# A decoder layer on one core: turned order of the group stage, one-hots in pairs, heads of a 32-token tile stacked on partitions

## The chip, the core and the metric

The kernel runs on one core of a Trainium2 chip. It is written in a tile framework: the program names operations on tiles, and the framework orders them and sets the semaphores. The metric is the device time of one execution in microseconds (us). Five engines matter. PE (TensorE) multiplies matrices; PEld is its weight load, which lies beside it. DVE (VectorE) does elementwise work and the top-k operations. ACT (ScalarE) does activations and copies with rounding. POOL (GpSimd) does elementwise work too and issues the indirect gathers. SP (SyncE) issues nearly all other transfers, in order. Each engine works through its own queue in order and waits on semaphores of the others.

## The reference, cut to what matters

There are 1056 tokens: 1024 of a prompt and 32 of a sample group (8 sequences of 4). The width is 1024, all in float32, one layer:

```python
z = rmsnorm(x) @ w_in                              # 1024 -> 2304 columns
h = x + concat([rwkv7(z_rwkv), pool_mix(z_pool)]) @ w_out   # 512 + 512 -> 1024
# PEER: product keys, 8 heads, 16 of 16384 single-neuron experts each
q  = (rmsnorm(h) @ wq).reshape(tokens, 8, 2, 128)
s1, s2 = q[:, :, 0] @ sub_keys[0].T, q[:, :, 1] @ sub_keys[1].T   # 128 scores each
v1, i1 = top_k(s1, 16);  v2, i2 = top_k(s2, 16)
sc, ci = top_k((v1[:, None] + v2[None, :]).flatten(), 16)
expert = i1[ci // 16] * 128 + i2[ci % 16];  gate = softmax(sc)
h = h + sum(gelu(u_tab[expert] @ hn) * gate * v_tab[expert])
h = h + (p @ w_ple) * sigmoid(rmsnorm(h) @ w_pg)
y = rmsnorm(h)
```

The RWKV part is a recurrence over the tokens of a sequence, the pooling part is not. Beside y the states are returned.

## The kernel before, in words

Activations lie transposed, width on the 128 partitions and tokens along the free axis. A float32 product of large matrices is done as three products of rounded halves, hi·hi + hi·lo + lo·hi, so each weight and each activation is split once: ACT rounds to hi, DVE or POOL subtracts to lo.

1. `phase_a` (from L189) multiplies the normalised input with the 18 column blocks of w_in. After each of the first products it calls `wsplit` (L176 to L187) twice: this loads four 128x128 blocks of a weight (`sraw`), splits them (`shi` on ACT, `slo` through the helper at L124 on POOL) and stores both to `wc_d` in DRAM. It does so for half of each w_out block (the half of the RWKV columns, 8 pieces) and all of wq (32 pieces), with one buffer for each of the three tiles. The pooling heads end in `yp_d`.
2. `bchunk` (L456 to L639) is the recurrence for 64 tokens; there are 16 such chunks and a sample chunk. Two chunks are in work at a time. A chunk's output goes to `y_d` (L639). `b_stream` runs a range of them.
3. The stage of the sample chunk and chunks 2 and 3. Behind it in program order stand `ple` (L981, the product p @ w_ple into `pl_d`) and `wpool` (L998): the pooled half of the out-projection for all tokens at once, x + w_out's second half times `yp_d`, in 8 blocks of three pieces of 352 columns, stored to `hx_d`.
4. `phase_c` (L682 to L751) for a group of tokens; the groups are 0 to 288, 288 to 544, 544 to 800 and 800 to 1056. It loads y and hx, splits y, adds w_out's RWKV half in 8 blocks (`mm3`, L655 to L664, K of 4 blocks), normalises (L712, L718), multiplies with 16 blocks of wq (K of 8) and with the keys (L747), and stores the scores to `sc_d` (L751). `wblock` (L641) loads the split weights back from `wc_d`, three buffers each of `whi` and `wlo`.
5. `top` and `select` (L753 to L853) for a tile of up to 128 tokens: for each of 8 heads, twice, the 16 best of 128 scores with their indices, then the 16 best of the candidates, codes and gates, with tokens on the partitions. The tokens below 672 are dense tiles: 128, 128 and 32 of group 0, 128 and 128 of group 1, 128 of group 2. For these the gates are spread into a matrix over all 16384 experts. `e12` holds the two halves of the expert's number; they and the gate are transposed (L863); for four tokens at a time a one-hot of each half is made (L875, on DVE, 1024 elements), the second one is multiplied with the gate's upper part (L877, DVE) and its lower part (`GLO`, on POOL for 110 of 168 and else on DVE), and two matmuls a token (L881) make the 128x128 matrix, which goes through `gst` to `g_d` (L884).
6. The remaining 384 tokens are three sparse tiles. Their top-k stands last (L1115). Then 768 gathers of expert rows (L1179) on POOL with a product each on DVE (L1187, L1196) run beside the dense experts: U blocks (`ublock`), gating (`ugate`) and V blocks (`vblock`), all with `esplit` (L1057 to L1064) and `emm` (L1069 to L1075).
7. The per-layer gate, the final norm and the stores.

The order is the program's: the framework plans with priority to what comes first in the program. `merge` interleaves several streams in proportion to given lengths. For the groups a loop (L1089) of four steps merges, in step s, the chunks of BC[s+1:s+3], the top-k and one-hots of group s-2 (`t_stream`), and `phase_c` of group s-1. In the last step `t_stream` of group 2 stands alone, and then `phase_c` of group 3 is merged with seven U blocks done ahead (`upre`).

The lines that the prediction speaks of most:

```python
ab = gp.tile([128, 3, EB, 4], F16, name="ab", bufs=3)               # L874
TT(ab[:, 0:2], iota16[:, None, :, :].to_broadcast([128, 2, EB, 4]), # L875
   e16[:, 0:2, None, t:t + 4].to_broadcast([128, 2, EB, 4]), op=ALU.is_equal)
mm(ps[:, i * 128:(i + 1) * 128], ab[:, k, :, i], ab[:, 0, :, i], start=k == 2, stop=k == 1)  # L881
```

Of the kernel before, what the change touches and what calls it, by code (L numbers as in the profile page):

```python
# [27 lines left out]
PB = 4  # L28
# [23 lines left out]
VG = 8  # L52

# [8 lines left out]
def body(ctx, tc, io):  # L62
# [12 lines left out]
    hx_d = dram.tile([128, KB, T], F32, name="hx_d")  # L75
# [4 lines left out]
    wc_d = dram.tile([KB + 16, 128, 2, KB, 128], F32, name="wc_d")  # L80
    xt_d = dram.tile([GT, D], F32, name="xt_d")
# [559 lines left out]
    def wblock(gi, b):  # L641
# [4 lines left out]
        for i in range(1 if b < KB else 2):  # L646
# [35 lines left out]
    def phase_c(gi):  # L682
# [7 lines left out]
        y = work.tile([128, 4, maxn], F32, name="y", tag="yp")  # L690
        nc.sync.dma_start(y[:, :, :n], y_d[:, :, c0:c1])
# [61 lines left out]
    def top(tk, pos, m):  # L753
        V12 = tk.tile([128, HEADS, 2, TOPK], F32, name="V12", bufs=1)
        I12 = tk.tile([128, HEADS, 2, TOPK], U32, name="I12", bufs=1)
# [13 lines left out]
        yield from select(tk, pos, m, V12, I12)  # L769


    def select(tk, col, m, V12, I12):
        NSL = HEADS * TOPK
        F12 = tk.tile([128, HEADS, 2, TOPK], F32, name="F12")
        for i in range(2):
            ACT(F12[:m, :, i, :], I12[:m, :, i, :], AF.Copy, scale=1.0 if i else 128.0)
        cand = tk.tile([128, HEADS, NCAND], F32, name="cand")
        code = tk.tile([128, HEADS, NCAND], F32, name="code")
        for src, dst, add in ((V12, cand, TT), (F12, code, PTT)):
            off = 0  # L780
            for a, b, w in SEG:
# [3 lines left out]
                if k == 1:  # L785
                    s1 = s1.to_broadcast([m, HEADS, w])
                elif w == 1:
                    s2_ = s2_.to_broadcast([m, HEADS, k])
                else:
                    o = o.rearrange("p h (k w) -> p h k w", w=w)  # L790
                    s1 = s1[:, :, :, None].to_broadcast([m, HEADS, k, w])
                    s2_ = s2_[:, :, None, :].to_broadcast([m, HEADS, k, w])
                add(o, s1, s2_, op=ALU.add)
                off += k * w
        PTT(code[:m], code[:m], iotaC[:m, None, :].to_broadcast([m, HEADS, NCAND]), op=ALU.add)
        SC = tk.tile([128, HEADS, TOPK], F32, name="SC")
        CI = tk.tile([128, HEADS, TOPK], U32, name="CI")
        s3 = cand
        for hh in range(HEADS):
# [153 lines left out]
    with tc.tile_pool(name="smp", bufs=1) as sp_, tc.tile_pool(name="hx", bufs=1) as hx:  # L953
# [73 lines left out]
        for st in (ple(), wpool()):  # L1027
            for _ in st:
                pass
# [349 lines left out]
```

## Time and profile before

| | |
|---|---|
| median of 3 runs | 3516.12 us (3502.51 to 3521.3) |
| the profiled execution's own time | 3494.25 us |
| its span (first to last instruction) | 3492.4 us |
| PE busy | 3262.7 us, 93% |
| DVE busy | 2675.0 us, 77% |
| POOL busy | 1769.3 us, 51% |
| ACT busy | 1179.8 us, 34% |
| HBM read, written | 759.22 MB, 120.60 MB |

How to read the profile. The page gives totals for each engine, and then the span in 40 slices of 87 us, each digit the busy share in tenths. A row of a group reads: line of the kernel, engine, operation, the tile written, the tiles read, the number of instructions, and then durations (minimum, median and maximum in nanoseconds, or busy microseconds and the mean), first and last start in microseconds, and the forms as partitions x elements. In the page's own group rows the last column is the idle time of the engine just before these instructions, and what ended it. A row of the waits reads: the waiting instruction, what released it, microseconds in all, how often, the longest. A row of a transfer ends with its size and the time from issue to landing. In the view by stretches of time every row gives, for each engine, its busy time and number of instructions in that stretch, then the granted clock of PE, the busy share of the DMA engines and what they moved.

### The profile page before, as it was taken

How to read it: one execution, taken by the hardware profiler on the slowest of the kernel's cores; microseconds unless marked ns; L12 is line 12 of the kernel's file. 1: busy time of each engine (PE TensorE's matmuls, PEld its weight loads, DVE VectorE, ACT ScalarE, POOL GpSimd, SP SyncE). 2: the span in 40 equal slices, each digit the busy share in tenths (PEclk: the TensorE clock that was granted, in tenths of full speed). 3: DMA queues.
4: the chain of work that ended last, by engine and by line, in shares of the span. 5: the costliest groups of instructions: out<-in, count | busy, mean ns of one | idle time of the engine just before them, and what ended most of it. 6: DMA issues, size and time to landing. Idle time of an engine off the chain costs nothing.

```text
span 3492.4 us, 57600 instructions
## 1 busy us (share of the span) xinstructions
PE 3262.7 (93%) x21831; PEld 3150.6 (90%) x21831; DVE 2675.0 (77%) x5366; ACT 1179.8 (34%) x1776; POOL 1769.3 (51%) x1433
## 2 busy tenths in 40 slices
PE   8997998999999899999999999999999999999997
PEld 7876998989989788999999999999999999999997
DVE  6767333279999799978788778878888787788866
ACT  6452424345556455322122122122122212222243
POOL 5434234145465454156656555555555565555635
PEclk9998999999999899999999999999999999999999
DMA  5667645767767867479888888889898898898834
GB/s 177 213 197 177 185 134 148 213 174 231 210 194 212 282 199 258 131 278 318 308 315 307 306 320 311 313 318 317 314 321 315 307 312 308 301 318 313 311 123 132
DMA packets 467861, 883.61 MB, mean 253 GB/s; under 512 B 129280, under 2 KB 252416, under 8 KB 463104
## 3 DMA queue, kind: packets, MB, share of 16 engines
q1 hardware_dynamic: 356992, 477.24, 43.5%
q0 software_dynamic: 110592, 402.70, 32.6%
q8 instruction: 171, 2.80, 0.3%
q14 instruction: 106, 0.87, 0.1%
HBM read 759.22 MB, written 120.60 MB: 252 GB/s over the span
## 4 chain that ended last, share of the span: by engine, by line
DMA 26%; PE 22%; DVE 19%; issue 14%; POOL 11%; ACT 1%; SPq 0%; POOLq 0%; DVEq 0%; ACTq 0%
DMA row<-v,idx 14%; POOL row L1179 10%; DMA row<-u,idx 7%; PE pd L1075 7%; PE ps L881 2%; DVE ab L875 2%; PE ps L663 2%; PE ps L661 2%; DVE row L1187 2%; PE ps L662 2%; DVE elo L1063 1%; DVE po L1196 1%; PE ps L526 1%; DVE ab L877 1%; DMA sraw<-wq 1%
## 5 line engine op out<-in xcount | busy, mean ns | idle before, releaser
L1179 POOL DMA_INDIRECT row<-u,idx x384 | 534.9, 1393 | 387.9 <-DVE row L1187 248.4
L1179 POOL DMA_INDIRECT row<-v,idx x384 | 520.5, 1355 | 377.3 <-DVE po L1196 222.4
L1196 DVE SCALAR_TENSOR_TENSOR po<-row,act,po 128x1024 f32<-128x1024 f32 x381 | 488.8, 1283 | 152.6 <-DMA row<-v,idx 147.8
L1187 DVE SCALAR_TENSOR_TENSOR row<-row,xt 128x1024 f32<-128x1024 f32 x384 | 463.6, 1222 | 179.4 <-DMA row<-u,idx 177.8
L1075 PE MATMUL pd<-XH,elo 128*128 128x336 f32 x2176 | 524.9, 323 | 52.2 <-DVE elo L1063 49.3
L1061 ACT ACTIVATE ehi<-eraw 128x1024 fp32r<-128x1024 f32 x278 | 293.0, 1054 | 750.3 <-PE pd L1075 676.1
L1075 PE MATMUL pd<-wh,elo 128*128 128x336 f32 (+1 forms) x2112 | 509.5, 320 | 31.2 <-DVE elo L1063 30.9
L1075 PE MATMUL pd<-XH,ehi 128*128 128x336 f32 x2176 | 518.0, 319 | 4.1 <-DVE OT L1150 2.3
L1075 PE MATMUL pd<-XL,ehi 128*128 128x336 f32 x2176 | 519.5, 320 | 0.0
L1075 PE MATMUL pd<-wh,ehi 128*128 128x336 f32 (+1 forms) x2112 | 506.5, 319 | 8.7 <-DVE tg L1260 6.3
L1075 PE MATMUL pd<-wl,ehi 128*128 128x336 f32 (+1 forms) x2112 | 504.3, 318 | 0.0
L1075 PEld LDWEIGHTS pd<-XH,elo 128*128 128x128 f32 x2176 | 376.9, 191 | 64.4 <-DVE elo L1063 61.5
L1075 PEld LDWEIGHTS pd<-wh,elo 128*128 128x128 f32 x2112 | 362.1, 189 | 40.1 <-DVE elo L1063 39.4
L1075 PEld LDWEIGHTS pd<-XH,ehi 128*128 128x128 f32 x2176 | 377.7, 192 | 5.1 <-ACT wt L1081 2.5
L1075 PEld LDWEIGHTS pd<-XL,ehi 128*128 128x128 f32 x2176 | 376.7, 191 | 0.2
L1075 PEld LDWEIGHTS pd<-wh,ehi 128*128 128x128 f32 x2112 | 364.2, 189 | 10.5 <-issue 8.4
L1075 PEld LDWEIGHTS pd<-wl,ehi 128*128 128x128 f32 x2112 | 364.3, 189 | 0.0
L1063 DVE TENSOR_TENSOR elo<-eraw,ehi 128x1024 fp32r<-128x1024 f32 x257 | 317.9, 1237 | 11.7 <-ACT ehi L1061 6.3
L1140 ACT ACTIVATE wh<-wt 128x672 fp32r<-128x672 f32 x128 | 97.5, 766 | 662.1 <-DVE wt L1138 662.1
L881 PE MATMUL ps<-ab 128*128 128x128 f16 x1344 | 195.9, 295 | 25.0 <-DVE ab L877 12.0
L124 POOL TENSOR_TENSOR ab<-ab,e 128x512 f16<-128x512 f16 x110 | 128.4, 1169 | 172.2 <-DVE ab L877 130.7
L882 ACT ACTIVATE gst<-ps 128x512 f32<-128x512 f32 x168 | 179.5, 1103 | 94.4 <-PE ps L881 92.5
(499 smaller groups left out, 5962.7 us busy)
## 6 DMA issues: line engine op xcount, KB each, us to landing
eraw<-uT SPq DMA_DIRECT2D x128, 512.0 KB, 5.4
eraw<-vP SPq DMA_DIRECT2D x128, 512.0 KB, 5.7
g_d<-gst SPq DMA_DIRECT2D x21, 2048.0 KB, 8.4
gq<-g_d SPq DMA_DIRECT2D x32, 1344.0 KB, 9.4
whi<-wc_d SPq DMA_DIRECT2D x148, 256.0 KB, 4.4
wlo<-wc_d SPq DMA_DIRECT2D x148, 256.0 KB, 4.7
wc_d<-shi SPq DMA_DIRECT2D x40, 256.0 KB, 2.6
wc_d<-slo SPq DMA_DIRECT2D x40, 256.0 KB, 3.1
```

Of the source, the lines that this page charges most:

```text
L124: nc.gpsimd.tensor_tensor(out, a, b, op=op)
L661: mm(ps[:, :n], whi[:, kk, :], xhi[:, k, :n], start=k == 0, stop=False)
L662: mm(ps[:, :n], whi[:, kk, :], xlo[:, k, :n], start=False, stop=False)
L881: mm(ps[:, i * 128:(i + 1) * 128], ab[:, k, :, i], ab[:, 0, :, i], start=k == 2, stop=k == 1)
L882: ACT(st[:, :, t2:t2 + 4].rearrange("p e t -> p t e"), v3(ps, 128), AF.Copy, scale=1.0 / GS)
L1061: ACT(hi, raw, AF.Copy)
L1063: sub(lo, raw, hi.bitcast(F32), op=ALU.subtract)
L1075: mm(ps[:, a, :n], w_[:, k, :], x_[:, s:s + n], start=first, stop=last)
L1140: ACT(wh, wt_, AF.Copy)
L1179: nc.gpsimd.indirect_dma_start(out=r[:m], out_offset=None, in_=io[tab], in_offset=bass.IndirectOffsetOnAxis(ap=idx[:m, hh, k:k + 1], axis=0))
L1187: STT(r[:m], r[:m], 1.0, xt[:m], op0=ALU.mult, op1=ALU.mult, accum_out=pre[:m, k:k + 1])
L1196: STT(po[:m], r[:m], act[:m, k:k + 1], po[:m], op0=ALU.mult, op1=ALU.add)
```

## The change

Four things are changed.

*The pooled half.* `wpool` and `hx_d` are gone. `wsplit` splits all of w_out, so there are 48 pieces. `phase_c` takes both halves at once: it loads `y_d` and `yp_d` one after the other into the same tile name, x straight into h, and the out-projection has K of 8 blocks, with two pairs of weight tiles for each block.

*The pools.* The tiles of `phase_c` and `top` (`ws`, `mv`, `work`, `tk`) are opened before the sample stage, and wait by tile rather than by pool. `ple` joins the merge with the sample chunk and chunks 2 and 3, and borrows the tiles `h`, `hi` and `lo`.

*The turned order.* `phase_c` of group 0 stands first and alone. Then, for groups 1 to 3, the chunks that the group needs are merged with `t_stream` of the group before, and `phase_c` of the group follows, alone, or for the last one merged with the seven U blocks. The chunks that were merged with a group's `phase_c` before now come behind it.

*Pairs and stacked heads.* The one-hots of four tokens are laid out as two pairs, so the two elements that stand side by side belong to two tokens and an operand of a matmul steps by two f16 elements instead of four; the comparison is two instructions of 512 elements instead of one of 1024. For the dense tile of 32 tokens four heads at a time stand below each other on 128 partitions (K = 4, H = 2): `top` loads four pieces of scores for one, and before the transposes the three rows of `e12` go through `e_d` in DRAM to bring the heads side by side again.

The diff, cut to its core:

```diff
     def wsplit(pool, b):
-        for i in range(0, HK if b < KB else KB, HK):
+        for i in range(0, KB, HK):
...
     def wblock(gi, b):
-        for i in range(1 if b < KB else 2):
+        for i in range(2):
...
     def phase_c(gi):
-        y = work.tile([128, 4, maxn], F32, name="y", tag="yp")
-        nc.sync.dma_start(y[:, :, :n], y_d[:, :, c0:c1])
         h = work.tile([128, KB, maxn], F32, name="h")
-        for d, s, L in segs(gi):
-            nc.sync.dma_start(h[:, :, d:d + L], hx_d[:, :, s:s + L])
...
-        for k in range(HK):
-            split(k, y[:, k, :n], yhi, ylo)
+        for part in range(2):
+            y = work.tile([128, 4, maxn], F32, name="y", tag="yp")
+            if part:
+                for d, s, L in segs(gi):
+                    nc.sync.dma_start(y[:, :, d:d + L], yp_d[:, :, s:s + L])
+                    nc.sync.dma_start(h[:, :, d:d + L], io["x"][:, :, s:s + L])
+            else:
+                nc.sync.dma_start(y[:, :, :n], y_d[:, :, c0:c1])
+            for k in range(HK):
+                split(part * HK + k, y[:, k, :n], yhi, ylo)
...
     def top(tk, pos, m):
-        for i in range(16):
+        K = HPS if m * HPS <= 128 and GA <= pos < GB else 1
+        H, n, m = HEADS // K, m, m * K
+        for i in range(2 * H):
             if i % 4 == 0:
-                nc.sync.dma_start(sq[:m], sc_d[TIDX[pos], :m, i:i + 4, :])
+                for j in range(K):
+                    nc.sync.dma_start(sq[j * n:(j + 1) * n], sc_d[TIDX[pos], :n, 2 * H * j + i:2 * H * j + i + 4, :])
...
+        ACT(e12[:m, 2, :NSL], gl[:m].rearrange("p a b -> p (a b)"), AF.Copy)
+        if K > 1:
+            for j in range(K):
+                nc.sync.dma_start(e_d[:, :, j * NSL:(j + 1) * NSL], e12[j * n:(j + 1) * n, :, :NSL])
+            e12 = tk.tile([128, 3, 128], F32, name="e12", tag="code")
+            nc.sync.dma_start(e12[:n], e_d)
+            m = n
...
-                ab = gp.tile([128, 3, EB, 4], F16, name="ab", bufs=3)
-                TT(ab[:, 0:2], iota16[:, None, :, :].to_broadcast([128, 2, EB, 4]),
-                   e16[:, 0:2, None, t:t + 4].to_broadcast([128, 2, EB, 4]), op=ALU.is_equal)
-                TT(ab[:, 2], ab[:, 1], e16[:, 2, None, t:t + 4].to_broadcast([128, EB, 4]), op=ALU.mult)
+                ab = gp.tile([128, 3, 2, EB, 2], F16, name="ab", bufs=3)
+                def pairs(j):
+                    return e16[:, j, t:t + 4].rearrange("p (a b) -> p a b", b=2)[:, :, None, :].to_broadcast([128, 2, EB, 2])
+                io16 = iota16[:, None, :, :].to_broadcast([128, 2, EB, 2])
+                for j in range(2):
+                    TT(ab[:, j], io16, pairs(j), op=ALU.is_equal)
+                TT(ab[:, 2], ab[:, 1], pairs(2), op=ALU.mult)
+                GLO(t)(ab[:, 1], ab[:, 1], pairs(3), op=ALU.mult)
...
-                        mm(ps[:, i * 128:(i + 1) * 128], ab[:, k, :, i], ab[:, 0, :, i], start=k == 2, stop=k == 1)
+                        mm(ps[:, i * 128:(i + 1) * 128], ab[:, k, i // 2, :, i % 2], ab[:, 0, i // 2, :, i % 2],
+                           start=k == 2, stop=k == 1)
...
-        merge([(30, bchunk(-1, ((sp_, ssm), bmask, cmask, spads))), (b_len(*BC[1:3]), b_stream(*BC[1:3]))])
-        for st in (ple(), wpool()):
-            for _ in st:
-                pass
+        merge([(30, bchunk(-1, ((sp_, ssm), bmask, cmask, spads))), (b_len(*BC[1:3]), b_stream(*BC[1:3])), (KB + 1, ple())])
...
-    for step in range(1, NG + 1):
-        streams = []
-        if step < NG:
-            c_ = BC[step + 1:step + 3]
-            streams.append((b_len(*c_), b_stream(*c_)))
-        if 0 <= step - 2 < NG:
-            streams.append((t_len(step - 2), t_stream(step - 2)))
-        if 0 <= step - 1 < NG:
-            streams.append((CL[step], phase_c(step - 1)))
...
+    for _ in phase_c(0):
+        pass
+    for gi in range(1, NG):
+        c_ = BC[gi + 1:gi + 3]
+        merge([(b_len(*c_), b_stream(*c_)), (t_len(gi - 1), t_stream(gi - 1))])
+        if gi < NG - 1:
+            for _ in phase_c(gi):
+                pass
+        else:
...
+            merge([(24, phase_c(gi)), (NPRE, upre())])
```

More of the change, by code (lines that the diff above doesn't have):

```diff
@@ L810, in select @@
         STT(s3[:m], s3[:m], -BIG, code[:m], op0=ALU.is_equal, op1=ALU.mult)
[L811 to L812 removed]
+        K16 = tk.tile([128, H, TOPK], F32, name="K16")
+        for hh in range(H):
             nc.vector.max(K16[:m, hh, 0:8], s3[:m, hh, :])
@@ L985, in ple @@
                 nc.sync.dma_start(wp, io["ple_w"][db])
-                hi, lo = split(sp_, wp, [128, 2, 128], "w", 2)
+                hi, lo = split(wp, *(sp_.tile([128, 2, 128], F32R, name=nm, bufs=2) for nm in ("whi", "wlo")))
                 pss = [PS("b3"), PS("b3"), PS("b2")]
```

137 lines of the change are left out of this document (53 added, 84 removed).

## The prediction, made before the result was known

> **What bounds the kernel now.** I read the page first (engine totals and the 40 slices), then busy time by stage, then the groups of the lines that change.
>
> ```profile
> span 3492.4 us, 57600 instructions
> PE 3262.7 (93%) x21831; PEld 3150.6 (90%) x21831; DVE 2675.0 (77%) x5366; ACT 1179.8 (34%) x1776; POOL 1769.3 (51%) x1433
> PE   8997998999999899999999999999999999999997
> DVE  6767333279999799978788778878888787788866
> DMA 26%; PE 22%; DVE 19%; issue 14%; POOL 11%; ACT 1%; SPq 0%; POOLq 0%; DVEq 0%; ACTq 0%
> ```
>
> No engine bounds the whole span: the chain passes through DMA, PE and DVE in turn. The DVE digits show the stage where the change acts: 3 in slices 5 to 8, then 9 and near it until slice 17. The next view gives busy time in stretches that I cut at events: first chunk, second chunk's end, group 0's loads, its normalised rows of group 1 (777), of group 2 (1034), of group 3 (1288), the first gathered expert row (1500), the last one (3319).
>
> ```profile
> core 0: us, PE busy (x) PEld busy (x) DVE busy (x) ACT busy (x) POOL busy (x), PEclk, DMA share, GB/s
> 0.00:316.00 316.00, 270.73 (x1382) 236.23 (x1383) 222.97 (x240) 157.98 (x273) 138.36 (x120) 0.95 0.62 201
> 316.00:412.00 96.00, 86.87 (x614) 83.19 (x612) 47.19 (x62) 42.40 (x83) 29.97 (x29) 0.94 0.66 162
> 412.00:554.00 142.00, 136.96 (x1055) 124.21 (x1054) 45.96 (x82) 41.45 (x81) 49.71 (x45) 1.00 0.50 135
> 554.00:777.00 223.00, 210.54 (x1673) 203.64 (x1674) 100.72 (x400) 89.91 (x187) 75.45 (x85) 0.98 0.66 186
> 777.00:1034.00 257.00, 241.83 (x1972) 233.18 (x1971) 247.20 (x960) 145.30 (x238) 143.62 (x142) 0.96 0.72 205
> 1034.00:1288.00 254.00, 232.80 (x1798) 220.20 (x1798) 229.99 (x850) 137.85 (x206) 129.88 (x128) 0.94 0.78 239
> 1288.00:1500.00 212.00, 199.23 (x1400) 192.00 (x1399) 199.82 (x893) 91.32 (x124) 73.34 (x80) 0.97 0.57 184
> 1500.00:3319.00 1819.00, 1732.54 (x11031) 1711.19 (x11030) 1469.36 (x1762) 399.91 (x489) 1055.18 (x768) 0.99 0.89 313
> 3319.00:3492.00 173.00, 151.19 (x919) 146.72 (x917) 111.80 (x122) 73.71 (x99) 73.75 (x42) 0.96 0.40 126
> ```
>
> Read DVE: 46 of 142 us before group 0, 101 of 223 while group 0 is projected, then 247 + 230 + 200 = 677 of 723 (94%) until the gathers begin. So from 777 to 1500 the top-k and one-hot work on DVE sets the pace; before that PE and the chunk recurrence do. From 1500 on, the expert rows and the dense experts run together with DMA at 0.89.
>
> ```profile
> L1179 POOL DMA_INDIRECT row<-u,idx x384: 932/1567/2445, 1499.8 to 3282.4; - x192
> ```
>
> **The frame of the sum.** In the program's order DVE has 15 weight subtractions (L1063) ahead of the first gathered row's product both before and after, and 228 against 229 between the first and the last one. So the work after the first gather is the same, and I keep its length: 3494.25 (this execution's own time; its span is 3492.4) less 1499.8 is 1994.4 us. The change moves the start of the gathers, and the three terms below say by how much.
>
> **Term A, until 777: the pooled half of the out-projection moves into the groups.**
>
> ```profile
> 1448.00:1500.00 52.00, 52.00 (x339) 52.00 (x338) 50.34 (x281) 15.02 (x21) 10.23 (x18) 1.00 0.25 72
> L1019 DVE TENSOR_TENSOR x<-ps,x x24: 511/524/525, 421.1 to 526.5; 128x352 f32<-128x352 f32 x24
> L691 SPq DMA_DIRECT2D y<-y_d x4: 556/566/623, 548.2 to 1195.0; - x4
> L712 PE MATMUL ps<-sa,ones x8: 377/380/483, 587.6 to 1271.8; 128*128 128x256 f32 x6, 128*128 128x288 f32 x2
> whi<-wc_d SPq DMA_DIRECT2D x148, 256.0 KB, 4.4
> wlo<-wc_d SPq DMA_DIRECT2D x148, 256.0 KB, 4.7
> ```
>
> Removed: the separate stage, 288 matmuls of 352 columns with their splits and stores (its additions, L1019, run from 421 to 527). Added: each of the 32 out-projection blocks takes 24 matmuls for 12, 384 more, 96 of them of 288 columns and 288 of 256; and two more 256 KB weight loads a block, 64 in all. By columns both are 101,376 (288 x 352; 96 x 288 + 288 x 256). The first row is a stretch in which PE does only matmuls of 336 columns: 52 us / 339 = 153 ns, 0.46 ns a column. So 46 us of PE leave the stretch to 527 and come back as 12 to 13 (33,792 or 25,000 columns a group) in four places. But group 0 cannot begin before chunk 3's output (its y load is issued at 548), and chunks 2 and 3 are a chain of small steps between which these matmuls were put. I let the chain gain a third of the 46, 15 us (y at about 533). Group 0's out-projection took 33 us (554 to the normalisation at 587.6). A weight buffer's round is 4.7 us to land and 12 matmuls of 288 columns (1.6 us) of use; three buffers make 2.1 us a half-block, so eight more half-blocks are +17 at most and nothing at least, where PE's own 33,792 columns (15.5 us) are partly hidden in the loads' waits; I take +5 here, and +6 for group 1's, which lies before 777 as well. A = -15 + 5 + 6 = -4. Its lower end is -46, all the PE time; its upper end comes from the weight splits:
>
> ```profile
> L181 SPq DMA_DIRECT2D sraw<-wq x32: 355/386/1105, 90.8 to 319.4; - x32
> L183 ACT ACTIVATE shi<-sraw x40: 613/632/654, 20.5 to 327.6; 128x512 fp32r<-128x512 f32 x40
> ACT shi L183 <- DMA sraw<-wq: 89.1, 22, 20.2
> L639 SPq DMA_DIRECT2D y_d<-yo x17: 526/552/4852, 402.1 to 1173.0; - x17
> ```
>
> Load, ACT round, POOL subtract and store have one buffer each, so the pieces form a chain: 31 steps from 90.8 to 319.4 are 7.4 us each, one of them with a wait of 20.2 (22 waits, 89.1 us on ACT). Eight more pieces move its end by 59, from some 330 to some 389. Behind the last piece stand, on SP, chunk 2's loads and the table of the per-layer embedding; on ACT and POOL, the chunks' rounds and masks. I cost this at nothing because chunk 0, whose output is stored at 402, covers it with 13 us to spare; without that cover it is up to +59, A's upper end.
>
> **Term B, DVE from 777 to 1500: stacked heads, pairs, and work drawn ahead.**
>
> ```profile
> L762 DVE MAX8 V<-scq x144: 262/275/297, 642.1 to 1462.7; 128x8 f32<-128x128 f32 x128, 32x8 f32<-32x128 f32 x16
> L1063 DVE TENSOR_TENSOR elo<-eraw,ehi 128x1024 fp32r<-128x1024 f32 x257 | 317.9, 1237 | 11.7 <-ACT ehi L1061 6.3
> L875 DVE TENSOR_TENSOR ab<-iota,e x168: 659/682/2708, 771.8 to 1363.4; 128x1024 f16<-128x1024 f16 x168
> L877 DVE TENSOR_TENSOR ab<-ab,e x168: 366/412/2326, 779.6 to 1365.5; 128x512 f16<-128x512 f16 x168
> L124 POOL TENSOR_TENSOR ab<-ab,e x110: 1029/1044/2404, 781.7 to 1366.1; 128x512 f16<-128x512 f16 x110
> sc_d<-scs SPq DMA_DIRECT2D x32, 256.0 KB, 4.7
> scq<-sc_d SPq DMA_DIRECT2D x32, 256.0 KB, 3.8
> ```
>
> Stacked heads: from 1448 to 1500 DVE does one tile's whole top-k, 50 us less some 7 weight subtractions of 1.24 us (339 matmuls are 7 blocks of 48), so 41. A 32-row instruction costs what a 128-row one does (262 to 297 over both forms). Two head steps in place of eight: -41 x 3/4, about -30. Against it come six more score loads of 3.8 us, which the two score buffers let run ahead of DVE, and a bounce through DRAM: a store of some 4.7 and a load of some 3.8, 9 us, which delay this tile's one-hots alone while another stream's instructions stand in between on DVE; uncovered they are +9. Pairs: one comparison of 1024 elements (682 ns) becomes two of 512; the product of that size takes 412, so 168 x (824 - 682) = +24. POOL keeps its 110 products of 1044. Net -6.
>
> The turned order starts group 0's top-k sooner. With each DVE instruction at its row's mean, added in the program's order, the work between the normalised rows of group 1 and of 2 is 250 us before and 235 after, between 2 and 3 229 and 274, from 3 to the first gather 201 and 122: 680 against 631. At the 94% pace the 49 would be 52. I don't take them: in the last part PE still has 178 (each matmul at its pitch from start to start), so PE paces it while it had waited in the part before: (235 + 274 + 178) / 0.94 = 731 against the measured 723. B is -10, for some of PE's slack at these joints; its ends are -52 and +33 (24 and the 9).
>
> **Term C, the pitch of the 1344 one-hot matmuls.**
>
> ```profile
> L881 PEld LDWEIGHTS <-ab x1344: 110/117/258, 780.4 to 1369.9; 128*128 128x128 f16 x192
> L881 PE MATMUL ps<-ab x1344: 272/297/330, 780.4 to 1370.1; 128*128 128x128 f16 x192
> L519 PEld LDWEIGHTS <-id x81: 96/98/152, 331.2 to 1140.4; 128*128 128x128 f16 x80, 64*64 64x64 f16 x1
> DVE ab L875 <- PE ps L881: 21.9, 18, 9.0
> ```
>
> Their operands step by 8 bytes; after, by 4. The nearest contiguous f16 weight load (L519) takes 98 where these take 117, so up to 19 ns x 1344 = 26 us of PE. The far end: 128 columns at term A's 0.46 ns are 58, and (117 - 58) x 1344 = 79. The other end is 0. In a stretch that DVE paces, PE time is worth what DVE waits for it (21.9 us) and what the joints of B give back: I take -15.
>
> The Trainium skill, page SBUF — State Buffer, section "Door 1: The DMA port swizzle", states 16-byte lines that need two or more hits for full rate. An 8-byte step has two already, so by that rule C is 0 and the sum -14; the trace's 117 against 98 speaks against it.
>
> **Sum.** -4 - 10 - 15 = -29 us, the gathers at 1471. This execution would be 3465; the median of the runs shown is 3516.12 (0.6% above this one), so 3487.
>
> **Rivals.**
> - *Hidden anyway.* A is nought and B's joints eat all: within 0.5%, which is about what a measurement of this kernel can tell from no change: 3516. For it: PE was 96 and 94% busy in the two stretches from 412 to 777. Against: 21.9 us of DVE waiting on these matmuls.
> - *The split chain decides (slower).* If the 48th piece is done after chunk 0's output (402), chunk 2's loads, in order behind it on SP, start late, nothing fills PE there any more, and the whole rest moves. From 9 us a piece (8 x 9 = 72 behind 330) it decides; two thirds of the 59 shown are +40: 3556. For it: one wait of 20.2 us and the first-come order on POOL. Against: the mean of 7.4 has that wait in it.
> - *PE was the coupled bound.* If the 4-byte step brings the 58 ns pitch, PE drops 79 us where it and DVE are level; then B's 52 and half of C's 79 come, -96 with A; the joints keep some, -80: 3436. For it: PE has 645 us of work for DVE's 631 after 777. Against: DVE digits of 9.
> - *Pairs lose the packed pace.* From the two rows, 512 elements more cost 270 ns. Were a run of two elements to halve the rate, 562 operations (336 comparisons, 168 products, 58 that POOL leaves to DVE) lose 270 each, 152 us on the pacing engine: 3640. The Trainium skill, page Vector Engine (DVE) Microarchitecture Reference, section 5.1, asks for 16-bit types, unit step and more than one innermost element, which pairs meet; no run here shows a run of two yet.
>
> **Chances.** Forecast case 0.35 (its own range 3460 to 3505), coupled 0.19, hidden 0.22, split chain 0.18, lost pace 0.06. Faster by over 0.5% is the first two less a little, 0.53; same 0.23; slower 0.24. The range leaves out the lost pace and some of each tail: 3405 to 3565.
>
> **What would show it.** A: group 0's y load near 533 for 548, the last split near 389. B: the 32-row forms gone, comparisons of 512 elements near 412, the first gather near 1471. C: the one-hot weight load below 117 and matmuls closer than 117 ns. Wrong if gathers still start at 1500 or later, if the length after them leaves 1994, or if comparisons take over 600.

## The result: slower, and the profile after

The changed kernel takes 3604.34 us in the median of 4 runs (3597.32 to 3608.57), the kernel before 3513.94 (4 runs): a ratio of 1.0258, 95% interval 1.0224 to 1.0292. I had forecast 3487 and a range up to 3565.

The page of the changed kernel, its totals and the slices of PE and DVE (90 us each):

```profile
span 3605.5 us, 57784 instructions
PE 3265.2 (91%) x21927; PEld 3139.7 (87%) x21927; DVE 2645.7 (73%) x5306; ACT 1175.1 (33%) x1791; POOL 1781.6 (49%) x1451
PE   8996899998888857999899999999999999999997
DVE  6776122279989896587788787887888788788766
```

PE is busy for as long as before (3265 for 3263), and DVE for 29 us less. The loss is time in which they wait: PE stands at 8 in the slices 10 to 14 and then at 5 and 7, DVE at 6 and 5 in the slices 16 and 17. The gathers, which I had expected at 1471, begin at 1600.6:

```profile
L1167 POOL DMA_INDIRECT row<-u,idx x384: 932/1534/1987, 1600.6 to 3394.8; - x192
```

That is 101 us later than in the profile before (1499.8). What follows takes 2005 us for 1993; in a second profile of the kernel before, the last of the experiments, it takes 2005 too.

Now the stretch between group 0's first load and the gathers, cut at the start of each group's y load and of the sum for its normalisation, at the last query block and at the first gather. The kernel before:

```profile
core 0: us, PE busy (x) PEld busy (x) DVE busy (x) ACT busy (x) POOL busy (x), PEclk, DMA share, GB/s
548.00:588.00 40.00, 36.44 (x284) 35.12 (x284) 10.20 (x22) 15.07 (x32) 17.53 (x19) 0.96 0.59 155
588.00:725.00 137.00, 130.49 (x1043) 126.61 (x1042) 44.51 (x145) 47.85 (x96) 32.04 (x30) 0.99 0.72 209
725.00:766.00 41.00, 36.05 (x287) 34.15 (x285) 36.88 (x198) 21.64 (x47) 27.12 (x35) 0.96 0.55 154
766.00:960.00 194.00, 184.80 (x1516) 179.97 (x1515) 184.89 (x714) 107.47 (x174) 100.05 (x97) 0.96 0.76 214
960.00:1020.00 60.00, 54.45 (x437) 51.13 (x435) 59.31 (x240) 33.11 (x57) 37.45 (x38) 0.97 0.63 180
1020.00:1195.00 175.00, 161.85 (x1346) 154.56 (x1346) 163.99 (x625) 98.76 (x158) 80.84 (x83) 0.99 0.76 231
1195.00:1271.00 76.00, 68.92 (x464) 63.08 (x463) 63.31 (x227) 40.83 (x53) 45.81 (x44) 0.83 0.83 260
1271.00:1400.00 129.00, 117.03 (x878) 109.70 (x877) 120.27 (x446) 67.39 (x93) 64.42 (x57) 0.96 0.71 234
548.00:1500.00 952.00, 887.41 (x6860) 851.42 (x6860) 779.61 (x3103) 465.59 (x755) 425.74 (x434) 0.96 0.69 205
```

The changed kernel, cut at the same events:

```profile
548.00:603.00 55.00, 50.54 (x380) 48.41 (x379) 11.40 (x24) 16.92 (x37) 25.50 (x28) 0.97 0.81 209
603.00:760.00 157.00, 142.18 (x1065) 135.96 (x1064) 58.87 (x303) 53.88 (x108) 31.95 (x37) 0.93 0.67 183
760.00:825.00 65.00, 60.03 (x492) 56.43 (x491) 53.90 (x212) 28.21 (x52) 35.79 (x39) 0.92 0.75 200
825.00:1017.00 192.00, 163.93 (x1500) 154.64 (x1497) 176.07 (x571) 108.82 (x176) 96.59 (x97) 0.95 0.81 228
1017.00:1084.00 67.00, 56.98 (x462) 54.67 (x460) 55.13 (x296) 30.33 (x59) 33.88 (x43) 0.90 0.81 209
1084.00:1288.00 204.00, 162.41 (x1415) 151.37 (x1412) 188.01 (x703) 106.44 (x169) 89.16 (x95) 0.88 0.77 228
1288.00:1390.00 102.00, 74.58 (x582) 68.78 (x583) 100.74 (x378) 44.49 (x61) 56.08 (x56) 0.88 0.70 219
1390.00:1500.00 110.00, 92.47 (x682) 87.45 (x680) 36.83 (x127) 37.31 (x58) 29.30 (x19) 0.95 0.68 225
548.00:1601.00 1053.00, 902.95 (x7208) 857.27 (x7207) 772.89 (x3081) 462.27 (x768) 419.03 (x444) 0.93 0.71 204
```

Read the last row of each first. PE does 903 us for 887, DVE 773 for 780, and the stretch is 101 us longer: PE stands idle for 150 us instead of 65, DVE for 280 instead of 172. Then read the stages in pairs. A stage from a y load to the normalisation (the out-projection) takes 55, 65, 67 and 102 us for 40, 41, 60 and 76. The stages between, in which the chunks of the next group are done, take 157, 192 and 204 for 137, 194 and 175. And where group 3's query blocks are done DVE is busy for 37 of 110 us, where it was busy for 120 of 129: it has run out of one-hots, and nobody has new scores for it.

The waits of PE in this stretch before (waiting instruction, what released it, us in all, how often, longest):

```profile
PE ps L881 <- DVE ab L877: 12.0, 14, 2.3
PE ps L661 <- DMA whi<-wc_d: 5.3, 4, 3.3
PE ps L663 <- DMA wlo<-wc_d: 1.3, 3, 0.6
```

and after, where the lines are L901, L662 and L664:

```profile
PE ps L901 <- DVE ab L897: 39.7, 25, 5.8
PE ps L662 <- DMA whi<-wc_d: 26.4, 16, 4.8
PE ps L664 <- DMA wlo<-wc_d: 11.2, 14, 1.8
PE ps L878 <- ACT e L868: 8.9, 3, 8.1
```

The waits of DVE before:

```profile
DVE V L762 <- DMA scq<-sc_d: 30.5, 6, 13.8
DVE wt L1138 <- DMA gq<-g_d: 4.9, 1, 4.9
```

and after:

```profile
DVE V L770 <- DMA scq<-sc_d: 96.1, 16, 17.5
DVE wt L1126 <- DMA gq<-g_d: 26.0, 1, 26.0
```

PE waits for one-hots (12 to 40 us) and for the doubled weight tiles (7 to 38), DVE waits for scores, which PE's projections make (31 to 96). Each engine waits for the other one in turn.

### The profile page after: what moved, and what is told of

It reads as the page before. It is cut to its first block, busy times and chain, and to the rows that moved or that the text cites. A ratio compares the mean times of both kernels' runs of the same rounds, so it can differ in the third digit from the quotient of the medians.

```text
span 3605.5 us, 57784 instructions
## 1 busy us (share of the span) xinstructions
PE 3265.2 (91%) x21927; PEld 3139.7 (87%) x21927; DVE 2645.7 (73%) x5306; ACT 1175.1 (33%) x1791; POOL 1781.6 (49%) x1451
## 4 chain that ended last, share of the span: by engine, by line
DMA 31%; PE 21%; DVE 20%; issue 14%; POOL 11%; ACT 2%; SPq 1%; POOLq 0%; DVEq 0%; ACTq 0%
DMA row<-v,idx 13%; DMA row<-u,idx 9%; POOL row L1167 8%; PE pd L1069 7%; DVE ab L896 3%; DMA sraw<-wq 2%; DVE row L1175 2%; DMA wlo<-wc_d 2%; PE ps L664 2%; PE ps L662 2%; PE ps L663 1%; DVE elo L1057 1%; POOL slo L125 1%; DVE ab L897 1%; DMA whi<-wc_d 1%
## 5 line engine op out<-in xcount | busy, mean ns | idle before, releaser
L1167 POOL DMA_INDIRECT row<-v,idx x384 | 533.1, 1388 | 398.7 <-DVE po L1184 230.5
L662 PE MATMUL ps<-hi,whi 128*128 128x256 f32 (+1 forms) x720 | 222.5, 311 | 36.3 <-DMA whi<-wc_d 26.4
L664 PE MATMUL ps<-hi,wlo 128*128 128x256 f32 (+1 forms) x720 | 221.4, 308 | 11.8 <-DMA wlo<-wc_d 11.2
```

The costliest lines, as they stand in the source:

```text
L662: mm(ps[:, :n], whi[:, kk, :], xhi[:, k, :n], start=k == 0, stop=False)
L664: l = mm(ps[:, :n], wlo[:, kk, :], xhi[:, k, :n], start=False, stop=k == K - 1)
L1167: nc.gpsimd.indirect_dma_start(out=r[:m], out_offset=None, in_=io[tab], in_offset=bass.IndirectOffsetOnAxis(ap=idx[:m, hh, k:k + 1], axis=0))
```

## The experiments

All times are medians; a ratio is to the kernel before on the same chip, with its 95% interval. "First gather" is the start of the gathers in the one profiled execution (1499.8 before); it leaves the long last part out. In nine profiles of kernels in which nothing is changed ahead of group 0's y load, that load is issued between 547 and 557 us, so a difference of less than 10 us in one first gather says little.

### The parts one by one

*The old order in the changed kernel.* The loop of the kernel before is put back:

```diff
-    for _ in phase_c(0):
-        pass
-    for gi in range(1, NG):
-        merge([(b_len(*c_), b_stream(*c_)), (t_len(gi - 1), t_stream(gi - 1))])
...
+    for step in range(1, NG + 1):
+        streams = [chunks of BC[step + 1:step + 3], t_stream(step - 2), phase_c(step - 1)]
...
```

> The changed kernel with the loop of the kernel before: in each step the chunks, the one-hots of the group before last and the projections of the last group are merged again. Everything else of the change stays. Theory 'order' (the turned loop makes the projections and the top-k take turns, so that DVE lies idle in group 3's projections): the 90 us go and the time is 3480 to 3520. Rival 'out-projection' (its double length in the groups and its double weight loads are the cost): 3570 to 3600. Rival 'one-hots' (pairs and stacked heads cost on DVE): 3570 to 3600 too; the next runs tell the two apart.

Measured: 3576.59, ratio 1.0197 (1.0149 to 1.0244), first gather 1579.2. The two rivals had this time. By the ratios some 21 us come back (the two intervals overlap) and 69 stay. The turned order is not the whole cause.

*The turned order alone*, in the kernel before: the loop of the changed kernel, nothing else.

> The kernel before with the turned loop alone. Theory 'order': 3590 to 3620 (the whole loss, and a little more for the top-k without stacked heads). Rival 'out-projection': 3520 to 3550. Both: somewhere between, by the share of each. In the profile, under 'order', DVE is busy for less than half of the time in which group 3's query blocks are done (37 of 110 us in the changed kernel, 120 of 129 before).

Measured: 3582.06, ratio 1.0215 (1.0181 to 1.0250), first gather 1576.9; the time lies between the two theories, as it would if both are at work. It costs about 75 us alone, and DVE has the hole at the end. Three stretches of this kernel, in the columns shown before: while chunks 6 and 7 are finished, while chunks 14 and 15 are finished, and group 3's query blocks:

```profile
708.00:764.00 56.00, 45.74 (x347) 42.77 (x345) 44.01 (x242) 24.58 (x49) 21.67 (x28) 0.91 0.34 83
1229.00:1281.00 52.00, 30.80 (x209) 28.55 (x207) 43.08 (x213) 22.23 (x39) 17.81 (x25) 0.69 0.64 200
1354.00:1473.00 119.00, 101.27 (x697) 94.81 (x696) 56.09 (x150) 41.63 (x62) 40.74 (x30) 0.91 0.68 216
```

PE is busy for 46 of 56 us and for 31 of 52. In the first of these it waits for the chunks' own steps (8.6 us, on ACT), in the second for the last chunk's step on POOL (6.6) and then for the next tile's top-k (12.2). Group gi's projections stand ahead of the next chunks in the program's order, are done first, and then little is left to lie between the steps of the recurrence. Before, chunks 4 to 7 ran beside group 0's projections, with PE busy for 130 of 137 us.

*The pooled half alone*, in the kernel before, in the old order:

```diff
-        for i in range(0, HK if b < KB else KB, HK):      # wsplit
+        for i in range(0, KB, HK):
-        for i in range(1 if b < KB else 2):               # wblock
+        for i in range(2):
-        for st in (ple(), wpool()):
+        for st in (ple(),):
... (and phase_c's head as in the changed kernel)
```

> The kernel before with the pooled half of the out-projection moved into the groups, in the old order, with the old one-hots and the old heads. Theory 'order': 3505 to 3530 (my term A, -4, with its cover holding). Rival 'out-projection': 3560 to 3600. Rival 'split chain': the same, with the sample chunk's and chunk 2's loads late.

Measured: 3598.24, ratio 1.0250 (1.0196 to 1.0303), first gather 1575.4. Against my term, which was -4, it alone costs about as much as the whole change. In its profile the four out-projections take 55, 64, 87 and 84 us for 39, 41, 60 and 77 before: 73 of the 76 us by which the first gather is late.

The split chain ended where I had forecast it (near 389): the last load is issued at 393.6, in the changed kernel at 393.4, and chunk 0's output is stored at 406 for 402. Group 0's y load is not late either. In the changed kernel:

```profile
L182 SPq DMA_DIRECT2D sraw<-wq x32: 364/383/1262, 159.0 to 393.4; - x32
L640 SPq DMA_DIRECT2D y_d<-yo x17: 545/560/7008, 406.4 to 1276.4; - x17
L701 SPq DMA_DIRECT2D y<-y_d x4: 563/568/577, 548.0 to 1288.0; - x4
```

But other loads stand behind the last piece on SP. The sample chunk's state and the first tables of `ple` are loaded at 411 to 412 us, where it was 353 to 354, and `ple`'s matmuls move with them. Before:

```profile
L985 SPq DMA_DIRECT2D wp<-ple_w x8: 328/414/769, 354.3 to 396.5; - x8
L991 PE MATMUL ps<-phi,whi x48: 320/323/641, 364.5 to 418.5; 128*128 128x352 f32 x48
412.00:548.00 136.00, 133.95 (x1034) 121.80 (x1034) 44.10 (x80) 40.25 (x78) 46.26 (x42) 1.00 0.48 133
```

and in the kernel with the pooled half alone:

```profile
L988 SPq DMA_DIRECT2D wp<-ple_w x8: 333/386/664, 412.5 to 447.7; - x8
L994 PE MATMUL ps<-phi,whi x48: 318/323/662, 425.0 to 493.3; 128*128 128x352 f32 x48
412.00:545.00 133.00, 122.02 (x923) 108.12 (x924) 36.45 (x59) 51.70 (x106) 55.53 (x52) 0.92 0.42 116
```

Of `ple`'s 144 matmuls 126 ran ahead of 412 us before; now all of them lie in the place that the 288 pooled ones left. PE is busy there for 122 of 133 us where it was for 134 of 136, and the way from chunk 0's output to group 0's y load is 8 us shorter (138 for 146; 142 in the changed kernel). So the cover that I had costed held for chunk 0 only. What the chain of chunks 2 and 3 would have given back with `ple` in its old place, no run shows.

*Pairs alone*, in the kernel before: the one-hots and the iota of the changed kernel.

> The kernel before with the one-hots in pairs alone. My terms: +24 us of DVE work, up to 26 us less on PE: 3500 to 3535. If pairs were the loss: over 3570. The weight loads of the one-hot matmuls at about 117 ns say that the step of 8 bytes cost nothing, at about 98 that it did.

Measured: 3538.42, ratio 1.0085 (1.0053 to 1.0116), first gather 1526.6; 3 us above my range. The matmuls of its one-hots, and DVE's comparisons (busy time, mean, then idle time before them):

```profile
L886 PEld LDWEIGHTS <-ab x1344: 96/97/209, 784.8 to 1395.4; 128*128 128x128 f16 x192
L886 PE MATMUL ps<-ab x1344: 217/218/330, 784.8 to 1395.4; 128*128 128x128 f16 x192
L881 DVE TENSOR_TENSOR ab<-iota,e x336: 392/414/2624, 776.9 to 1392.3; 128x512 f16<-128x512 f16 x168
L881 DVE TENSOR_TENSOR ab<-iota,e 128x512 f16<-128x512 f16 x336 | 185.4, 594 | 13.4 <-PE ps L886 13.3
```

Weight loads fall from 117 to 97 ns, and from start to start the matmuls fall from 118 to 58 ns (medians over neighbours): 80 us less of PE by that pitch. The busy time of these matmuls falls by 66 us (130 for 196), and the idle time ahead of them grows by 46 (71 for 25), most of it spent waiting for DVE's products. The comparisons have the median that I forecast (414), and DVE has 185 us of them for 147: in all it is busy 805 us for 780 up to the first gather. So what PE saves becomes waiting. The first gather is 27 us later, about as much as DVE has more work; that the one is the reason for the other is not shown, since with eight tokens at a time (below) it is as late with DVE busy for less.

*Stacked heads alone*, in the kernel before: `top` and `select` of the changed kernel with the old one-hots.

> The kernel before with the heads of the 32-token tile stacked, nothing else. My term: 30 us less of DVE, with a bounce of 9 us that other work covers: 3480 to 3505 if DVE paces its stretch. If the chain of chunks and projections paces it and DVE only keeps up, 3505 to 3515. If the extra score loads or the bounce stand on the path, above 3520.

Measured: 3526.68 over 10 runs, ratio 1.0064 (1.0040 to 1.0087), first gather 1514.8, of which 6 us lie ahead of any change (chunk 0's output at 407 for 401). DVE has 22 us less up to the gathers (758 for 780; I had forecast 30), and nothing of it is seen in the time. The time lies where the third theory had it, but the rows don't show its reason: DVE waits for scores 36 us for 31, and no engine is seen to wait for the bounce. While group 3's query blocks are done (1281 to 1411) DVE is now busy for 104 of 130 us where it was for 120 of 129: the work that was taken away had been the work that lay beside PE.

### What in the pooled half costs

*Its weight loads left out*, and *its matmuls left out*, both in the kernel with the pooled half alone:

```diff
-        for i in range(2):                                # first kernel: no loads
+        for i in range(1 if b < KB else 2):
-            mm3(ps, w, (yhi, ylo), n)
+            mm3(ps, w + w, (yhi, ylo), n)
```

```diff
-            mm3(ps, w, (yhi, ylo), n)                     # second kernel: no matmuls
+            mm3(ps, w[:1], (yhi, ylo), n)
```

> The pooled half in the groups alone (as in the run with 3598), but its second twelve matmuls of a block use the first half's weights again, so that the 64 more weight loads are gone; the out-projection is wrong thereby. Theory 'matmuls moved from a place where they were free': 3575 to 3600, nothing gained. Theory 'weight loads': 3505 to 3535.

> The pooled half in the groups alone, with all its loads and splits, but without its 384 matmuls (the pooled half is left out of the result). Theory 'matmuls moved from a place where they were free': 3510 to 3545. Theory 'weight loads': 3570 to 3600.

Measured: without the loads 3572.17, ratio 1.0188 (1.0137 to 1.0240), first gather 1563.9; without the matmuls 3560.00, ratio 1.0153 (1.0106 to 1.0201), first gather 1540.8. Neither theory: of the 76 us by which the first gather is late, leaving out the loads gives back 12 and leaving out the matmuls 35, and with the matmuls gone 41 us are still there, some 32 of them in the four out-projections (43, 49, 70 and 88 us). By the medians it is 24 and 36 us, and the interval of each overlaps that of the pooled half alone, so these shares are rough.

*The pooled half taken first.* In the changed kernel both halves of y go through one tile, so the second load waits for the splits of the first: ACT begins to split the first half at 553, 765, 1025 and 1296 us and the second at 562, 782, 1038 and 1307. The data of the pooled half is there long before, so here it is loaded, split and multiplied first:

```diff
-        for part in range(2):
+        for part in (1, 0):
-        for i in range(2):                                # wblock
+        for i in (1, 0):
-        for k in range(K):                                # mm3
+        for j in range(K):
+            k = (j + HK) % K
... (and the same exchange for the last group's blocks of wq)
```

> The pooled half in the groups alone, but with that half taken first: its load, its splits and its matmuls stand ahead of those of the recurrence's half. In the run with 3598 the second load of a group begins only when the splits of the first have freed the one tile (9 to 17 us from the first half's split to the second's in the changed kernel). Theory 'the single tile makes a second hop behind every group's last chunk': 3550 to 3575, four hops of about 10 us gone. Theory 'only matmuls and weight loads count': 3585 to 3605, no change.

Measured: 3565.23, ratio 1.0164 (1.0119 to 1.0208), first gather 1551.2. The same helper serves the pooling heads' own projection, whose halves are exchanged by this edit, so their values are other ones; the instructions are the same in number and shape. 24 us come back. Chunk 0's output comes 12 us earlier (391 for 403), which the edit may have caused through that helper, but at group 0's y load only 2 of these are left (543 for 545). From y load to normalisation the four groups take 46, 61, 74 and 79 us for 55, 64, 87 and 84, 30 less in all: a second hop of 3 to 13 us is there. The stages between them take 16 us more. The same edit in the changed kernel:

> The changed kernel with the pooled half taken first in the same way. Theory 'second hop': 3560 to 3585. Theory 'only matmuls, loads and the turned order count': 3595 to 3610.

Measured: 3617.91, ratio 1.0298 (1.0258 to 1.0337), first gather 1599.5, above both theories, and here its out-projections are shorter too (50, 66, 50 and 95 us for 55, 65, 67 and 102), but two of the stages between grow (166, 206 and 203 us for 158, 192 and 204), and nothing is won: group 3's y load is issued at 1288 us in both. What holds the chunks there was not found.

### What in the turned order costs

*The chunks one group ahead*, in the kernel with the turned order alone:

```diff
-    for _ in phase_c(0):
-        pass
+    merge([chunks 4 to 7, phase_c(0)])
     for gi in range(1, NG):
-        c_ = BC[gi + 1:gi + 3]
+        c_ = BC[gi + 2:gi + 4]          # none for gi = 3
```

> The kernel before with the turned loop alone, as in the run with 3582, but with the chunks one group ahead: chunks 4 to 7 are merged with group 0's projections, and those of group 2 and 3 with the one-hots of group 0 and 1, so that each group's chunks are done when its projections begin; one-hots and projections still take turns. Theory 'the chunks stand behind the projections and have nothing beside them to fill PE': 3505 to 3535. Theory 'one-hots and projections take turns': 3560 to 3590.

Measured: 3543.35, ratio 1.0106 (1.0086 to 1.0126), first gather 1559.5. By the medians half of the loss of 1.0215 goes, which neither theory had. In the two profiled executions (the slowest of this kernel, the fastest of the other) the first gather comes only 17 us earlier: the stages between the out-projections take 568 us for 611, and the last one, from group 3's normalisation to the first gather, 251 for 223. So the place of the chunks is a part of the cause, between a fifth and a half of it. That the rest comes from projections and one-hots in turn is argued from the waits, and no run shows it by itself.

### Do the parts add up?

> The changed kernel with the old one-hots and unstacked heads, so the turned order and the pooled half together. Alone they cost 71 and 88. If they add up: 3650 to 3670. If they lengthen the same chain of chunks and projections, and pairs and heads count for little there: 3590 to 3615. If pairs cost 25 there as they do alone: 3570 to 3590.

> The change without the pooled half: the separate stage stays, with the turned order, pairs and stacked heads. If costs add up (71 + 28 + 19): 3620 to 3640. If the pooled half adds nothing to the turned order: 3595 to 3610. If it adds its own 20 to 30: 3570 to 3590.

The first is the changed kernel with the old one-hots and HPS = 1; the second is the kernel before with the turned loop, pairs and stacked heads. Measured: 3614.98, ratio 1.0302 (1.0269 to 1.0335), first gather 1603.4, at the upper end of the second theory; and 3565.10, ratio 1.0178 (1.0153 to 1.0204), first gather 1554.0, below all three. All that was run of the parts, by ratio:

| | old one-hots and heads | pairs and stacked heads |
|---|---|---|
| neither | 1 | pairs alone 1.0085, heads alone 1.0064 |
| turned order | 1.0215 | 1.0178 |
| pooled half | 1.0250 | 1.0197 |
| both | 1.0302 | 1.0258 (the change) |

The rows differ in one thing more. The early pools, with `ple` in the merge, are in both kernels of the last row and in the one with 1.0197, and in no other; they were not run alone, so what they cost or bring is open.

The parts do not add up: turned order and pooled half cost 1.0215 and 1.0250 alone and 1.0302 together. The stages say where. The turned order alone makes the stages between the out-projections longer (611 us in all for 506), the pooled half alone the out-projections (290 for 217). Together the out-projections keep their 70 us (287), but the stages between grow by 46 only (553). Pairs and stacked heads cost where they stand alone, and in all three rows below the figure is lower with them by about 0.4 to 0.5%, though in each row the two intervals overlap.

### Three smaller questions

*Eight tokens at a time.* If DVE and PE only count together, pairs must not cost DVE anything. The kernel before, with stacked heads, and one-hots in pairs for eight tokens, in three tiles of their own (`oc` with one buffer) and with the matmuls of eight tokens in two rounds:

```diff
+ TT(ob, io16, pairs(1), op=ALU.is_equal)       # io16, pairs: [128, 4, EB, 2], 1024 elements
+ TT(oa, io16, pairs(0), op=ALU.is_equal)
+ TT(oc, ob, pairs(2), op=ALU.mult)
+ GLO(t)(ob, ob, pairs(3), op=ALU.mult)
```

> The kernel before with stacked heads and pairs made for eight tokens at a time: two comparisons of 1024 elements and one product of 1024 on DVE for eight tokens (2 x 682 + 682 = 2046 ns where the kernel before takes 2 x (682 + 412) = 2188 and the changed one 2 x (2 x 415 + 412) = 2484), and the 4-byte step that took the matmuls' pitch from 118 to 58 ns. Theory 'DVE and PE are coupled' (either alone gives little, both together the gain of both): 3430 to 3470. Theory 'DVE alone paces': 30 for the heads and 12 for the one-hots: 3465 to 3480. Theory 'the chain of chunks and projections paces': 3495 to 3515.

Measured: 3533.33, ratio 1.0063 (1.0032 to 1.0094), first gather 1526.2 (9 us of it ahead of the change: chunk 0's output at 410). None of the three. From the first load to the gathers PE is busy for 845 of 969 us and DVE for 773, so DVE lost only 6 of the 42 us that I had worked out from the medians, and the 42 us that PE is busy less (887 before) are idle time: ahead of the one-hot matmuls it is 55 us for 25.

*The products off POOL.* DVE's one-hot instructions have means far above their medians. In the kernel before all products go to DVE (`GLO` returns the DVE one):

> The kernel before with the 110 one-hot products of POOL done on DVE. In the profile of before the comparisons have a median of 682 ns and a mean of 885, the products 412 and 551: 69 us of the 276 us of DVE's one-hot work lie above the medians. Theory 'DVE is held while POOL works on its products': the medians hold, DVE's one-hot work is 253 to 260, and the time is 3490 to 3515. Theory 'the long ones come from elsewhere': 45 us more on DVE, 3540 to 3560.

Measured: 3518.34 over 10 runs, ratio 1.0016 (0.9999 to 1.0034), first gather 1506.0; between the two theories. Its groups:

```profile
L875 DVE TENSOR_TENSOR ab<-iota,e 128x1024 f16<-128x1024 f16 x168 | 125.7, 756 | 14.6 <-PE ps L881 13.4 <-ACT e L866 0.4
L878 DVE TENSOR_TENSOR ab<-ab,e 128x512 f16<-128x512 f16 x168 | 84.2, 511 | 0.2
L877 DVE TENSOR_TENSOR ab<-ab,e 128x512 f16<-128x512 f16 x168 | 81.6, 497 | 0.1
```

110 instructions with a median of 416 ns came to DVE, 46 us, and its one-hot work grew by 18 only (292 us for 273): the comparisons' mean fell from 885 to 756 ns. So the work on POOL does lengthen them, but not alone: the means still lie above the medians of 684 and 415. What else lengthens them was not tried.

*The kernel before, once more.*

> The kernel before once more, for a second profile. The gathers last 1816 to 1843 us in the profiles so far, 1818 in the one of before. If the changes lengthen them by their own doing, they last 1815 to 1822 here; if this is the spread from execution to execution, 1825 to 1840 is as likely.

Measured: 3503.26, first gather 1496.6, and the gathers last 1829.7 us, 12 more than in the first profile. Up to the gathers these two profiles of one kernel agree within 3 us. Since the gathers of one kernel differ by 12 us, I read nothing from the 1816 to 1862 us that they take in all the profiles; some of it may be the changes' own doing.

## Why the prediction was wrong, by its own steps

- **The frame** (the gathers' start decides, what follows keeps its length) held: 101 us of the profiles' 113 lie ahead of the first gather.
- **Term A, -4, was the largest error.** The pooled half alone costs 2.5%, 76 us at the first gather. The step that failed is the price of the work in the groups: "+5 here, and +6" for groups 0 and 1, whose out-projections grew by 16 and 23 us in that run (15 and 24 in the changed kernel), and no price at all for groups 2 and 3, since DVE was to pace them, which grew by 27 and 8. The "15 us" that the chain of chunks 2 and 3 was to give back failed too: y came 3 us earlier in that run and not at all in the changed kernel. What the groups pay is not matmuls only (35 us of 76) nor loads (12), but also that the second half comes behind the first through one tile. Work was moved to the head of four groups, where the next chain waits for it.
- **A slip in term A:** group 0's out-projection has 96 matmuls of 288 columns, 27,648 and not 33,792, which is 12.7 us of PE and not 15.5. Nothing hangs on it.
- **The split chain**, my slower rival, came about in part. Its end was at 393 for the forecast 389, and chunk 0's output, the cover, came only 4 us later. But "I cost this at nothing" looked at chunk 0 alone. The loads of the sample chunk and of `ple`, which stand behind the last piece, came 58 us later, nearly the 59 that I had worked out, and `ple`'s matmuls filled the place that the pooled ones had left. The rival's price (the whole rest moves by 40) was not paid, since group 0's y load was not late.
- **Term B: the work was right and its worth wrong.** I had DVE 6 us lighter in net, and it is 7 lighter (773 for 780), comparisons at 416 ns for 412. The step that failed is (235 + 274 + 178) / 0.94 = 731: between the ends of the normalised rows (844, 1103 and 1405 us) and the first gather the three parts took 259, 302 and 196, 756 in all. From 1084 to 1390 DVE was busy for 289 us of 306 while PE was idle for 69, and from 1390 to 1500 DVE was idle for 73 of 110. I had seen that PE and DVE would pace in turn; I kept 0.94 for whichever one paces, as if the other one's work could always be put beside it. With the order turned it could not.
- **The turned order had no price ahead of 777.** Term A counted only the pooled half there. With the turned order alone group 1's sum for its normalisation comes at 812 us for 767, which is 45 of the 77 us by which its first gather is late (5 of them stand already at group 0's y load): chunks 4 to 7 no longer run beside group 0's projections.
- **The 94% of DVE was read as a bound.** PE was 93% busy in the same stretch (674 of 723 us), and both depended on three streams being merged. Taking 22 us from DVE alone brought nothing (heads alone), and what pairs alone took from PE became waiting. Making a nearly full engine lighter makes a thing faster only if the others let it.
- **Term C, -15, had the wrong size and the wrong worth.** The far end came true, 58 ns from start to start for 118, 80 us of PE by the pitch, but in pairs alone it brought nothing. The rival "PE was the coupled bound" rested on just that, and gave 3436. By the Trainium skill, page SBUF — State Buffer, section "Door 1: The DMA port swizzle", two hits in a line of 16 bytes are enough, and an 8-byte step has two; the measured pitch says that for these f16 matmuls they are not. The rule's result for the sum (C at nought) was nearer to the truth all the same, by luck.
- **The lost packed pace** did not come: two neighbours in the innermost run keep 414 to 416 ns for 512 elements.
- **What was missing** is a rival: that projections, chunks and one-hots, once in turn, leave each engine idle in the other one's part. With the turned order alone this is worth about 75 us. Its mark was in the profile before: the stage of group 3's query blocks with DVE at 120 of 129 us, beside PE at 117.

What stays open: how the pooled half's rest of 41 us (without its matmuls) is shared among the second hop, the loads and the doubled splits; what the early pools do; what the chain of chunks 2 and 3 would take without `ple` in it; why pairs and heads seem to help a little beside the other parts; and what lengthens DVE's one-hots besides POOL.

No kernel that was run is faster than the one before.

## What to carry to other kernels

When several streams are merged so that two engines are both over 90% busy, that share is a property of the order and no bound of either engine: ask of every move what lies beside the work at its old place and at its new one, stage by stage, for both engines. A chain of small steps needs other work beside it that fills the engine's gaps. Work that is moved to the head of a chain is paid there, and with it come its loads and the hop of its own data (76 us here for matmuls worth 46). Where a queue works in order, look at everything that stands behind a chain that grows, and not only at the first thing. Compare idle time of each engine in the same stage, not busy totals.

## What the runs showed of the hardware

- A step of 4 instead of 8 bytes in the f16 operands took weight loads from 117 to 97 ns and the pitch of 128-column matmuls from 118 to 58 ns.
- DVE's f16 comparisons of 1024 elements have a median of 682 ns and a mean of 885 beside POOL's products, 684 and 756 without them.
- PE's granted clock is lower where PE waits more: 0.93 from 548 us to the gathers in the changed kernel for 0.96 before, and 0.69 in the 52 us in which the turned order alone leaves it 31 us of work. The matmuls of the projections keep their median pitch (119 and 120 ns for 256 columns). But the chunks' matmuls of 64 columns (L588) last 421 ns in those 52 us, where they last 275 before (316 to 412 us, clock 0.94). So the lower clock goes with the idle time, and may itself lengthen a chain; how much was not tried.
